# An fp32 two-block network on one core: the start's loads in halves and on a second queue, the shift as columns, the first expert activations ahead of the last score

## The chip, the core and the metric

The kernel runs on one core of one Trainium2 chip. Its engines are TensorE (PE; weight loads are listed apart as PEld), VectorE (DVE), ScalarE (ACT), GpSimd (POOL) and SyncE (SP), each with a queue of its own that it works off in order, and 16 DMA engines. SP, ACT and POOL issue DMAs. The metric is the device time in microseconds, the median of three runs.

## The reference, cut to what matters

Two blocks run one after the other in fp32 on 512 tokens of width 1024. The first has a modulation, windowed attention, a gated convolution and a mixture of 16384 experts of rank 1, of which each token takes 8 x 16. The second has two layers, each with a mixer, cross attention over a memory of 256 tokens, and an MLP. The parts that the change touches:

```python
# modulation: one row for the tokens (c), one for the context (c_ctx)
m = silu(cond) @ w_mod + b_mod            # shift, scale, gate, shift, scale, gate
h  = rmsnorm(x,  n1) * (1 + sc1)  + sh1
hc = rmsnorm(xc, n1) * (1 + csc1) + csh1
...
# experts
qh = (t @ w_q).reshape(T, 8, 2, 128)
s = einsum('thpd,hpnd->thpn', qh, sub_keys)   # scores of the sub-keys
s_top, i_top = top_k(s, 16)
...
act = gelu(einsum('thkd,td->thk', u_tab[idx], t))
y = einsum('thk,thkd->td', g * act, v_tab[idx])
...
# second block
kv = mem @ mem_w_kv                        # once, for both layers
o = softmax(q @ mem_k.T / 16) @ mem_v
x = layer_norm(ALPHA * x + o @ wo)
```

## The kernel before

**Products.** Every weight comes from HBM as fp32 into one of two buffers named `raw` (`wload`, L73; the load is L81) and is split into a high part `wh` and a rest `wl`: ACT casts (L68), DVE subtracts (L69), 1024 columns at a time. Activations are split in the same way. Each product then takes three matmuls, L93 to L95. In a transposed product (`fm`) the weights are the stationary operand, in the other (`tm`) the activations.

**Order.** The Python text names the operations; a scheduler then fixes each engine's own order, and semaphores join the engines. So the order of a queue differs from the order of the text, and an edit in one place can move rows of other engines. The DMAs that SP and ACT issue share eight semaphores in turn, so an issue can also wait for the DMA that had its semaphore before.

**The start.** The keys and values of the memory (`mem_kv`, c = 0 to 7, result `pskv`, copied to `kv` by ACT at L326 and stored) are computed while the modulation is loaded. The first product needs the split memory `mt` and the split weights of c = 0. Between the products stands a loop over four quarters. Each loads `w_mods` (1 MB) and `w_modh` (1 MB) into the two buffers `wm`. The scale comes from DVE: `gemv` at L217 multiplies `w_mods` by the broadcast rows `crow` and `ccrow` and adds up, four times a quarter. The shift comes from PE: L358 has `cc` (the two conditions, 2 columns) as stationary operand and streams 512 columns of `w_modh`, in two PSUM tiles `gv`. Then come `mem_kv(1 + c)` and 128 tokens of x: load, scaling by their norm on ACT, eight transposes into `psT` (L339), copies into `xn`. Behind the loop the shift's two rows are copied (`mrow`), turned into columns by eight transposes (`pssh`, L372), and `xn` is modulated on DVE (L344) and split into `h`. Then c = 5, 6, 7 (called kv5, kv6, kv7 below), the context, and the projections of the first block.

**The experts.** `score` makes, for each pair of a head and a half, the matmuls `pss` of queries `pq` (split) and keys, and transposes the scores (`psst`); DVE takes the 16 best (`top`). Behind the last `score`, a loop over c loads the table's rows `peer_u[c]`, multiplies them by `h` (`psu`), and writes gelu of it to HBM (`actd`, store at L791 on SP). Rows chosen by index come by indirect DMAs that POOL issues (`rows`, L749); DVE takes dot products with them at L732. Gates are placed by one-hot products (`oh`, L1049, and `pg`, L1025) and stored (`gd`, L1035 on SP). A DMA issue on SP holds up what stands behind it until its source is ready.

**Cross attention.** `xattn` runs four heads, then `tm_stage` loads the out-projection `xo` and multiplies (`tm`).

Of the kernel before, what the change touches and what calls it, by code (L numbers as in the profile page):

```python
# [9 lines left out]
F32 = mybir.dt.float32  # L10
F32R = mybir.dt.float32r
# [4 lines left out]
AF = mybir.ActivationFunctionType  # L16
# [4 lines left out]
P = 128  # L21
T = 512
NT = 4
D = 1024
KT = 8
# [6 lines left out]
ND = T - NG  # L32
NE = ND // P
WCOLS = 1032
# [8 lines left out]
class Net:  # L43
# [130 lines left out]
    def tm_stage(self, X, wsrc, evac, side, nwp=2):  # L174

        with self.pool("wx", side=side, bufs=8 - 2 * nwp) as wx:
            w = [self.wload(wsrc[c], wx if c >= nwp else None) for c in range(4)]
            for t in range(NT):  # L180
                for half in range(2):
                    ps = self.psa.tile([P, 512], F32, tag="a", name=f"tm{t}")
                    for c in range(2):
                        self.tm(ps, w[2 * half + c], X, t, nk=4, k0=4 * c, width=512, start=c == 0, stop=c == 1)
                    if half == 1:
                        self.flush()
                    evac(t, half, ps)
# [45 lines left out]
    def front(self):  # L233
# [53 lines left out]
        with self.pool("start", side="right") as sp, self.pool("start2", side="right", bufs=2) as sp2, \  # L287
# [16 lines left out]
            nc.sync.dma_start(crow, i["c"].partition_broadcast(P))  # L304
            nc.sync.dma_start(ccrow, i["c_ctx"].partition_broadcast(P))
            nc.scalar.activation(crow, crow, AF.Silu)
            nc.scalar.activation(ccrow, ccrow, AF.Silu)
            nc.sync.dma_start(modb, i["b_mod"])
            nc.sync.dma_start(bhc, i["b_row"])
            nc.sync.dma_start(b1c, i["b_col"])  # L310
            nc.sync.dma_start(n1c, i["norm1_g"])
            nc.sync.dma_start(n2c, i["norm2_g"])
            wm_es = ExitStack()
            wmp = wm_es.enter_context(self.pool("wm", side="right", bufs=2))
            gv = [self.psa.tile([P, 512], F32, tag="a", name=f"gv{b}") for b in range(2)]
            def mem_kv(c, pool, tag):
                w = w_kv.pop() if w_kv else self.wload(i["mem_w_kv"][c])
                ps = pool.tile([P, 512], F32, tag=tag, name="pskv")
                for j in range(2):
                    o = ps[:, j * 256 : (j + 1) * 256]  # L320
                    if c < 4:
                        self.fm(o, w, j, MT, cols=slice(0, 256))
                    else:
                        self.tm(o, w, MT, j)
# [22 lines left out]
            for c in range(4):  # L347
# [19 lines left out]
            mrow = sp2.tile([P, D], F32, tag="xt", name="mrow", bufs=3)[:2]  # L367
            for b in range(2):
                nc.scalar.copy(mrow[:, b * 512 : (b + 1) * 512], gv[b][:2])
            ps = self.psc.tile([P, 512], F32, tag="c", name="pssh")  # L370
# [264 lines left out]
    def peer(self):  # L635
# [38 lines left out]

        with self.pool("qk", side="right", bufs=2) as qp, self.pool("keys", side="right") as kp:
# [31 lines left out]
            for hp in range(16):  # L707
# [12 lines left out]
                last = (hp, q)  # L720
            score(*last)
# [57 lines left out]

        def u_matmuls(w, a, tile_):  # L780
            for j in range(2):
                ps = tile_()
                self.fm(ps[:, :ND], w, j, H2, cols=slice(0, ND))
                nc.scalar.activation(a[:, j * ND : (j + 1) * ND], ps[:, :ND], AF.Gelu)

        G0 = 12
        for c in range(C1):
            w = self.wload(i["peer_u"][c])
            a = uact.tile([P, 2 * ND], F32, tag="act", name="act")
            u_matmuls(w, a, lambda: self.psa.tile([P, 512], F32, tag="a", name="psu"))  # L790
            nc.sync.dma_start(actd[c], a)  # L791
# [146 lines left out]
    def routing(self, VAL, IDX, GT, iota_n, iota_a, first_a, u1, u2, gd, ids, gg):  # L938
# [81 lines left out]
        def expand(oh, gs, b, dst):  # L1020
# [13 lines left out]
            if b == 1:  # L1034
                nc.sync.dma_start(dst, gs.rearrange("p (b n) t -> p b (n t)", b=16))  # L1035
# [315 lines left out]
    def xattn(self, l):  # L1351
# [4 lines left out]
        with self.pool("xa", side=other, bufs=2) as xp, self.pool("xa4", side=other, bufs=4) as xp4:  # L1356
# [55 lines left out]
            for h in range(4):  # L1412
                p1 = scores(Q, kv, 1)
# [17 lines left out]
        self.tm_stage(O, i["xo"][4 * l : 4 * l + 4], evac, other)  # L1431
# [226 lines left out]
```

## Time and profile before

| | before |
|---|---|
| median of 3 runs | 2922.74 us (2921.97 to 2922.75) |
| the profiled execution's own time | 2922.15 us |
| its span in the trace | 2920.3 us |
| PE busy | 2878.6 us, 99% of the span |
| DVE, ACT, POOL busy | 69%, 44%, 13% |

The profile is of one execution. Its span leaves out 1.9 us around the program. Shares are means over stages that differ: 99% for PE says that the other engines are a limit only in the short stretches in which PE waits or has its lower clock.

### The profile page before, as it was taken

What the parts mean: (1) busy time and instruction counts of PE and PEld (TensorE: products, weight loads), DVE (VectorE), ACT (ScalarE), POOL (GpSimd) and SP (SyncE); (2) the same over time, 40 slices, a digit from 0 to 9 for tenths busy, and PEclk for the clock granted to TensorE, in tenths of its full rate; (3) what the DMA queues carried; (4) which work ended last, traced back from release to release, by engine and by line L of the source; (5) the groups of instructions that cost most, each with busy time, mean ns of one, the idle gap of its engine ahead of it and who ended that gap; (6) DMA issues with size and microseconds to landing.
All of it is one profiled execution on the core that took longest, in us unless ns stands there. A gap on an engine that the chain in (4) does not pass through costs nothing.

```text
span 2920.3 us, 39527 instructions
## 1 busy us (share of the span) xinstructions
PE 2878.6 (99%) x15409; PEld 2482.8 (85%) x15409; DVE 2016.5 (69%) x3823; ACT 1279.8 (44%) x1910; POOL 367.5 (13%) x283
## 2 busy tenths in 40 slices
PE   7999999999999999999999999999999999999998
PEld 5887888899999989988888889888888889888887
DVE  6887658989768688888888884766433456643345
ACT  5565334456556333333333365644433334433332
POOL 0000000000101355454444200000000000000000
PEclk9999999999999999999999999999999999999999
DMA  8312642257889999999999722223322222322221
GB/s 323 127 44 104 228 159 101 98 209 229 278 270 298 354 362 357 344 343 392 387 368 364 263 79 102 108 94 110 116 93 102 89 99 80 105 92 99 101 75 70
DMA packets 163402, 556.21 MB, mean 190 GB/s; under 512 B 13712, under 2 KB 62992, under 8 KB 131984
## 3 DMA queue, kind: packets, MB, share of 16 engines
q1 hardware_dynamic: 125200, 417.37, 40.1%
q0 software_dynamic: 36864, 134.23, 12.4%
q8 instruction: 120, 1.97, 0.3%
q10 hardware_dynamic: 1152, 2.10, 0.2%
q14 instruction: 66, 0.54, 0.1%
HBM read 504.90 MB, written 48.76 MB: 190 GB/s over the span
## 4 chain that ended last, share of the span: by engine, by line
PE 87%; DVE 6%; issue 3%; DMA 3%; ACT 1%; POOL 0%; SPq 0%; DVEq 0%; ACTq 0%; POOLq 0%
PE ps L95 8%; PE ps L93 8%; PE ps L94 8%; PE po L93 6%; PE po L94 6%; PE po L95 6%; PE psu L93 3%; PE psu L94 3%; PE psu L95 3%; PE tm L93 2%; PE tm L94 2%; PE tm L95 2%; PE pu L95 2%; PE pu L93 2%; PE pu L94 2%
## 5 line engine op out<-in xcount | busy, mean ns | idle before, releaser
L69 DVE TENSOR_TENSOR wl<-raw,wh 128x1024 fp32r<-128x1024 f32 x538 | 652.2, 1221 | 273.4 <-ACT wh L68 259.8
L68 ACT CAST wh<-raw 128x1024 fp32r<-128x1024 f32 x538 | 559.0, 1048 | 633.2 <-PE ps L95 228.5
L94 PE MATMUL po<-wl,ga 128*128 128x512 f32 x768 | 302.9, 394 | 0.0
L93 PE MATMUL po<-wh,ga 128*128 128x512 f32 x768 | 302.7, 394 | 0.0
L95 PE MATMUL po<-wh,ga 128*128 128x512 f32 x768 | 302.5, 394 | 0.0
L749 POOL DMA_INDIRECT rows<-in_u_rows,ids x128 | 171.6, 1341 | 599.2 <-DVE rows L732 398.7
L93 PE MATMUL psu<-h,wh 128*128 128x384 f32 x704 | 241.3, 343 | 0.0
L94 PE MATMUL psu<-h,wh 128*128 128x384 f32 x704 | 239.0, 339 | 0.0
L95 PE MATMUL psu<-h,wl 128*128 128x384 f32 x704 | 238.8, 339 | 0.0
L749 POOL DMA_INDIRECT rows<-in_peer_v,ids x128 | 186.1, 1454 | 229.9 <-DVE acc L742 216.3
L95 PE MATMUL ps<-wh,hg 128*128 128x512 f32 x512 | 201.8, 394 | 0.0
L93 PE MATMUL ps<-wh,hg 128*128 128x512 f32 x512 | 201.7, 394 | 0.0
L94 PE MATMUL ps<-wl,hg 128*128 128x512 f32 x512 | 201.2, 393 | 0.0
L68 ACT CAST ga<-m 128x384 fp32r<-128x384 f32 x128 | 65.5, 513 | 268.5 <-DVE m L835 120.6
L94 PE MATMUL ps<-xt,wh 128*128 128x512 f32 x448 | 176.9, 395 | 0.0
L93 PE MATMUL ps<-xt,wh 128*128 128x512 f32 x448 | 176.8, 395 | 0.0
L95 PE MATMUL ps<-xt,wl 128*128 128x512 f32 x448 | 176.5, 394 | 0.0
L95 PEld LDWEIGHTS po<-wh,ga 128*128 128x128 f32 x768 | 144.2, 188 | 34.1
L93 PEld LDWEIGHTS po<-wh,ga 128*128 128x128 f32 x768 | 144.1, 188 | 33.3
L94 PEld LDWEIGHTS po<-wl,ga 128*128 128x128 f32 x768 | 144.1, 188 | 33.2
L732 DVE SCALAR_TENSOR_TENSOR rows<-rows,hrow 128x1024 f32<-128x1024 f32 x128 | 154.8, 1219 | 20.4 <-DMA rows<-in_u_rows,ids 20.4
L742 DVE SCALAR_TENSOR_TENSOR acc<-rows,dots,acc 128x1024 f32<-128x1024 f32 x127 | 162.9, 1283 | 0.4
(542 smaller groups left out, 6651.5 us busy)
## 6 DMA issues: line engine op xcount, KB each, us to landing
raw<-in_peer_u SPq DMA_DIRECT2D x64, 1024.0 KB
raw<-in_peer_v SPq DMA_DIRECT2D x64, 1024.0 KB
raw<-in_w SPq DMA_DIRECT2D x64, 1024.0 KB
gd<-gs SPq DMA_DIRECT2D x24, 1024.0 KB
g<-gd SPq DMA_DIRECT2D x16, 1536.0 KB
raw<-in_w_in SPq DMA_DIRECT2D x17, 1024.0 KB
actd<-act SPq DMA_DIRECT2D x44, 384.0 KB
a<-actd SPq DMA_DIRECT2D x44, 384.0 KB
```

The source lines that it names most:

```text
L68: self.nc.scalar.copy(h, src)
L69: self.nc.vector.tensor_sub(l, src, h.bitcast(F32))
L93: mm(ps, a[0], b[0], start=start, stop=False)
L94: mm(ps, a[0], b[1], start=False, stop=False)
L95: mm(ps, a[1], b[0], start=False, stop=stop)
L732: keep(nc.vector.scalar_tensor_tensor(r, r, 1.0, self.hrow, op0=ALU.mult, op1=ALU.mult, accum_out=dots[:, j : j + 1]))
L742: keep(nc.vector.scalar_tensor_tensor(acc[0], r, dots[:, j : j + 1], acc[0], op0=ALU.mult, op1=ALU.add))
L749: nc.gpsimd.indirect_dma_start(out=r, out_offset=None, in_=i["u_rows"] if n < P else i["peer_v"], in_offset=bass.IndirectOffsetOnAxis(ap=i ...
```

## The change

Six edits. The memory and the first weights are loaded in two halves each, in turn on SP, and split half by half; the product c = 0 takes the halves in that order. The eight small loads (the conditions, also as broadcast rows, biases and norms) are issued by ACT. The shift is computed as columns: `w_modh` is the stationary operand, 128x128 at a time, and `cc` the two moving columns, in one PSUM tile, with no transposes behind. The first `u_matmuls` (c = 0) stand ahead of the last `score`. The stores of `act` and of the gates `gs` are issued by ACT. Two loads of `xo` are named inside the last head.

```diff
-    def tm_stage(self, X, wsrc, evac, side, nwp=2):
+    def tm_stage(self, X, wsrc, evac, side, nwp=2, w=()):
...
-            w = [self.wload(wsrc[c], wx if c >= nwp else None) for c in range(4)]
+            w = list(w) + [self.wload(wsrc[c], wx if c >= nwp else None) for c in range(len(w), 4)]
...
-            mraw = self.rawp.tile([P, 2048], F32, tag="raw", name="memt")
-            nc.sync.dma_start(mraw, i["mem"])
+            for dst, src in ((cc, "cc"), (modb, "b_mod"), (bhc, "b_row"), (b1c, "b_col"), (n1c, "norm1_g"), (n2c, "norm2_g")):
+                nc.scalar.dma_start(dst, i[src])
+            for dst, src in ((crow, "c"), (ccrow, "c_ctx")):
+                nc.scalar.dma_start(dst, i[src].partition_broadcast(P))
+
+            mraw, kraw = (self.rawp.tile([P, 2048], F32, tag="raw", name=nm) for nm in ("memt", "raw"))
+            w_kv = [[]]
             for j in range(2):
-                v = mraw[:, j * 1024 : (j + 1) * 1024].rearrange("p (k m) -> p k m", k=4)
+                js = slice(j * 1024, (j + 1) * 1024)
+                nc.sync.dma_start(mraw[:, js], i["mem"][:, js])
+                nc.sync.dma_start(kraw[:, js], i["mem_w_kv"][0][:, js])
+            for j in range(2):
+                js = slice(j * 1024, (j + 1) * 1024)
+                v = mraw[:, js].rearrange("p (k m) -> p k m", k=4)
                 self.split(MT[0][:, 4 * j : 4 * j + 4], MT[1][:, 4 * j : 4 * j + 4], v)
-            w_kv = [self.wload(i["mem_w_kv"][0])]
-            nc.sync.dma_start(cc, i["cc"])
+                w_kv[0].append(tuple(self.wp.tile([P, WCOLS], F32R, tag=f"w{z}", name=f"w{z}") for z in "hl"))
+                self.split(w_kv[0][j][0][:, :1024], w_kv[0][j][1][:, :1024], kraw[:, js])
...
+                if c == 0:
+
+                    for x in range(16):
+                        k, j = x // 8 * 4 + x % 4, x // 4 % 2
+                        s, (wh, wl) = slice(k % 4 * 256 + j * P, k % 4 * 256 + (j + 1) * P), w[k // 4]
+                        self.mm3(o[j], (wh[:, s], wl[:, s]), (MT[0][:, k], MT[1][:, k]), x == 0, x == 15)
+                for j in range(2 if c else 0):
...
-                for b in range(4):
-                    k = 2 * c + b // 2
-                    nc.tensor.matmul(gv[b % 2][:2], cc[:, k], raw[:, b * 512 : (b + 1) * 512], start=k == 0, stop=k == 7)
+                for b in range(16):
+                    k, f = 2 * c + b // 8, b % 8
+                    nc.tensor.matmul(
+                        gv[:, 2 * f : 2 * f + 2], raw[:, b * P : (b + 1) * P], cc[:, k], start=k + f == 0, stop=k + f == 14)
...
-            for k in range(KT):
-                nc.tensor.transpose(ps[:, 2 * k : 2 * k + 2], mrow[:, k * P : (k + 1) * P], self.ident[:2, :2])
-            nc.vector.tensor_add(shc, ps[:, :16].rearrange("p (k z) -> p k z", z=2), bhc[:, :, None].to_broadcast([P, 8, 2]))
+            nc.vector.tensor_add(shc, gv[:, :16].rearrange("p (k z) -> p k z", z=2), bhc[:, :, None].to_broadcast([P, 8, 2]))
...
+        def activations(c):
+            w = self.wload(i["peer_u"][c])
+            a = uact.tile([P, 2 * ND], F32, tag="act", name="act")
+            u_matmuls(w, a, lambda: self.psa.tile([P, 512], F32, tag="a", name="psu"))
+            nc.scalar.dma_start(actd[c], a)
...
+            activations(0)
             score(*last)
...
-            nc.sync.dma_start(actd[c], a)
+            if c:
+                activations(c)
...
-                nc.sync.dma_start(dst, gs.rearrange("p (b n) t -> p b (n t)", b=16))
+                nc.scalar.dma_start(dst, gs.rearrange("p (b n) t -> p b (n t)", b=16))
...
+                if h == 3:
+                    wo = [self.wload(i["xo"][4 * l + c]) for c in range(2)]
```

The edits move rows of the engines. The first place is DVE's queue around the copy of `xn` for the last quarter of x. Each `wl<-raw,wh` is the subtract of half a weight block. Before, from the last norm of x on:

```order
L69 TENSOR_TENSOR wl<-raw,wh 128x1024 x2
L162 TENSOR_SCALAR rms_850<-rms_ss 128x1
L361 COPY xn<-psT 128x4x128
L373 TENSOR_TENSOR shc<-pssh,bhc 128x16
L344 TENSOR_SCALAR xn<-xn,scc,shc 128x512 x6
L69 TENSOR_TENSOR h_114<-xn,h_113 128x1024 x3
L344 TENSOR_SCALAR xn<-xn,scc,shc 128x512 x2
L69 TENSOR_TENSOR wl<-raw,wh 128x1024 x2
L69 TENSOR_TENSOR h_114<-xn,h_113 128x1024
L69 TENSOR_TENSOR wl<-raw,wh 128x1024 x2
```

The first `wl` pair there is that of kv5, the others those of kv6 and kv7. The same place after the change:

```order
L165 SCALAR_TENSOR_TENSOR rms_651<-rms_652,rms_651 128x1
L370 COPY xn<-psT 128x4x128
L352 TENSOR_SCALAR xn<-xn,scc,shc 128x512 x6
L69 TENSOR_TENSOR h_114<-xn,h_113 128x1024 x3
L352 TENSOR_SCALAR xn<-xn,scc,shc 128x512 x2
L69 TENSOR_TENSOR wl<-raw,wh 128x1024 x2
L69 TENSOR_TENSOR h_114<-xn,h_113 128x1024
L69 TENSOR_TENSOR wl<-raw,wh 128x1024 x2
```

Now the pairs behind the copy are those of kv5 and kv6: kv5's has moved from ahead of the copy to behind the modulates, and PE has one product more to run behind them.

The second place is SP's queue in the loop over quarters; the semaphores in brackets name the engine that an issue waits for (DMAHW is one of the eight shared by the DMAs). Before, quarters 1 and 2:

```order
L349 DMA wm<-in_w_mods 128x2048 [waits DMAHW7_49,DMAHW2_49,DVE_49]
L355 DMA wm<-in_w_modh 128x2048 [waits DMAHW3_49,DMAHW0_49,PE_49]
L81 DMA raw<-in_mem_w_kv 128x2048 [waits DMAHW1_49,Activation_49]
L333 DMA xt<-in_x 128x1024
L349 DMA wm<-in_w_mods 128x2048 [waits DMAHW7_49,DMAHW4_49,DVE_49]
```

After:

```order
L81 DMA raw<-in_mem_w_kv 128x2048 [waits DMAHW3_49,DMAHW0_49,DVE_49]
L357 DMA wm<-in_w_mods 128x2048 [waits DMAHW5_49,DMAHW2_49,PE_49]
L363 DMA wm<-in_w_modh 128x2048 [waits DMAHW4_49,DVE_49]
L341 DMA xt<-in_x 128x1024
L81 DMA raw<-in_mem_w_kv 128x2048 [waits DMAHW6_49,DVE_49]
L357 DMA wm<-in_w_mods 128x2048 [waits DMAHW7_49,DMAHW3_49,PE_49]
```

The two buffers `wm` have changed roles from quarter to quarter: `w_mods` now takes the one that PE's `gv` frees, `w_modh` the one that DVE's `gemv` frees, and the next weights of the memory product (`raw`) stand ahead of the pair instead of behind it.

The third place is PE's queue at the last score. Before, the last `pss` stands three matmuls behind the transposes of the score before:

```order
L93 MATMUL pss<-pq_5471,kh_4394 128x512
L95 MATMUL psu<-h_3917,wl 128x384
L699 MATMUL psst<-ident,sf 128x128 x4
L93 MATMUL psu<-h_3917,wh 128x384
L94 MATMUL psu<-h_3918,wh 128x384
L95 MATMUL psu<-h_3917,wl 128x384
L94 MATMUL pss<-pq_5472,kh_4394 128x512
L95 MATMUL pss<-pq_5471,kl_4395 128x512
```

After, behind the transposes and the 41 `psu` matmuls that follow them:

```order
L93 MATMUL psu<-h_3954,wh 128x384
L94 MATMUL psu<-h_3955,wh 128x384
L95 MATMUL psu<-h_3954,wl 128x384
L93 MATMUL pss<-pq_5508,kh_4431 128x512
L94 MATMUL pss<-pq_5509,kh_4431 128x512
L95 MATMUL pss<-pq_5508,kl_4432 128x512
```

So all of the first `psu` block stands ahead of the last `pss` now. Behind this block PE's rows are the same as before, and from the cross attention on so are those of every engine but for the numbers of DMA semaphores.

## Rows read from the trace of the kernel before

**Rows 1.** The page: busy time, share, instructions.

```profile
PE 2878.6 (99%) x15409; PEld 2482.8 (85%) x15409; DVE 2016.5 (69%) x3823; ACT 1279.8 (44%) x1910; POOL 367.5 (13%) x283
```

**Rows 2.** What PE waited for: us in total, times, longest us.

```profile
PE pskv L93 <- ACT wh L68: 11.2, 3, 9.4
...
PE tm L93 <- ACT wh L68: 2.8, 2, 1.4
...
PE pss L94 <- DVE pq L69: 3.5, 2, 2.9
...
PE pg L1025 <- DVE oh L1049: 2.5, 3, 1.9
```

**Rows 3.** Table by stretches: us, busy of each engine, PEclk, DMA share, GB/s.

```profile
20.00:60.00 40.00, 35.69 (x208) 23.26 (x207) 28.91 (x55) 21.43 (x31) 0.00 (x0) 1.00 0.91 335
...
558.00:570.00 12.00, 9.07 (x44) 8.41 (x43) 11.50 (x63) 4.58 (x6) 0.00 (x0) 0.86 0.25 88
...
765.00:785.00 20.00, 17.71 (x113) 17.25 (x113) 17.15 (x28) 12.02 (x16) 3.97 (x3) 0.91 0.82 259
...
1000.00:1600.00 600.00, 600.00 (x2802) 514.73 (x2802) 512.77 (x657) 212.82 (x294) 289.40 (x204) 1.00 0.96 364
```

**Rows 4.** Timeline of the start: start us, us, engine, line, operation.

```profile
0.74 1.28 ACT L68 ACT_TABLE_LOAD   x1 [0.74 <-PEq L1648]
...
5.81 1.99 ACT L68 CAST mt<-memt 128x1024 fp32r<-128x1024 f32 x2 [3.79 <-DMA memt<-in_mem]
...
10.67 0.58 PE L95 MATMUL pskv<-mt,wl 128*128 128x256 f32 x1 [0.47 <-DVE wl L69]
...
18.80 0.59 ACT L326 COPY kv<-pskv 128x512 f32<-128x512 f32 x1 [5.08 <-PE pskv L95]
```

**Rows 5.** Timeline of PE: `gv`, `pssh`, and `psd` much later.

```profile
42.60 3.59 PE L358 MATMUL gv<-wm,cc 128*2 128x512 f32 x8
...
65.56 0.65 PE L372 MATMUL pssh<-ident,mrow 2*128 2x2 f32 x8
...
2402.25 0.29 PE L1525 MATMUL psd<-band,x 128*128 128x16 f32 x2
...
2402.70 0.29 PE L1525 MATMUL psd<-band,x 128*128 128x16 f32 x2
```

**Rows 6.** Timeline of the loop: `w_mods` issued on SP, first used on DVE.

```profile
32.49 0.33 SPq L349 DMA_DIRECT2D wm<-in_w_mods  x1
...
39.89 1.22 DVE L217 SCALAR_TENSOR_TENSOR junk<-wm,crow 128x1024 bf16<-128x1024 f32 x1 [1.67 <-DMA wm<-in_w_mods]
...
44.96 0.33 SPq L349 DMA_DIRECT2D wm<-in_w_mods  x1
...
49.78 1.23 DVE L217 SCALAR_TENSOR_TENSOR junk<-wm,crow 128x1024 bf16<-128x1024 f32 x1
```

**Rows 7.** Timeline behind the loop: PE, DVE and ACT.

```profile
64.59 1.03 PE L339 MATMUL psT<-ident,xt 128*128 128x128 f32 x8
...
73.61 2.35 DVE L69 TENSOR_TENSOR wl<-raw,wh 128x1024 fp32r<-128x1024 f32 x2
...
74.88 0.39 PE L94 MATMUL pskv<-wl,mt 128*128 128x256 f32 x1 [0.80 <-DVE wl L69]
...
86.31 0.59 ACT L326 COPY kv<-pskv 128x512 f32<-128x512 f32 x1 [0.55 <-PE pskv L95]
```

**Rows 8.** Timeline at the last score: DVE and PE.

```profile
546.60 1.20 DVE L69 TENSOR_TENSOR wl<-raw,wh 128x1024 fp32r<-128x1024 f32 x1
...
559.67 1.21 DVE L69 TENSOR_TENSOR wl<-raw,wh 128x1024 fp32r<-128x1024 f32 x1
...
561.53 0.50 PE L94 MATMUL pss<-pq,kh 128*128 128x512 f32 x1 [2.93 <-DVE pq L69]
```

**Rows 9.** What SP waited for, and DVE from 560 to 800 us.

```profile
SPq L791 <- ACT act L784: 181.5, 37, 11.2
...
DVE rows L732 <- DMA rows<-in_u_rows,ids: 17.3, 4, 7.7
```

More of the change, by code (lines that the diff above doesn't have):

```diff
@@ L300, in front @@
                 self.split(MT[0][:, 4 * j : 4 * j + 4], MT[1][:, 4 * j : 4 * j + 4], v)
-            w_kv = [self.wload(i["mem_w_kv"][0])]
-            nc.sync.dma_start(cc, i["cc"])
+                w_kv[0].append(tuple(self.wp.tile([P, WCOLS], F32R, tag=f"w{z}", name=f"w{z}") for z in "hl"))
+                self.split(w_kv[0][j][0][:, :1024], w_kv[0][j][1][:, :1024], kraw[:, js])
             nc.scalar.activation(cc, cc, AF.Silu)
-            nc.sync.dma_start(crow, i["c"].partition_broadcast(P))
@@ L305, in front @@
-            nc.sync.dma_start(ccrow, i["c_ctx"].partition_broadcast(P))
             nc.scalar.activation(crow, crow, AF.Silu)
             nc.scalar.activation(ccrow, ccrow, AF.Silu)
[L308 to L312, printed above, removed]
             wm_es = ExitStack()
             wmp = wm_es.enter_context(self.pool("wm", side="right", bufs=2))
-            gv = [self.psa.tile([P, 512], F32, tag="a", name=f"gv{b}") for b in range(2)]
+            gv = self.psa.tile([P, 512], F32, tag="a", name="gv")
@@ L318, in mem_kv @@
                 ps = pool.tile([P, 512], F32, tag=tag, name="pskv")
-                for j in range(2):
-                    o = ps[:, j * 256 : (j + 1) * 256]
+                o = [ps[:, j * 256 : (j + 1) * 256] for j in range(2)]
+                if c == 0:
[4 more added lines that the diff above has]
+                for j in range(2 if c else 0):
                     if c < 4:
-                        self.fm(o, w, j, MT, cols=slice(0, 256))
+                        self.fm(o[j], w, j, MT, cols=slice(0, 256))
                     else:
-                        self.tm(o, w, MT, j)
+                        self.tm(o[j], w, MT, j)
                 kv = sp2.tile([P, 512], F32, tag="kv", name="kv")
@@ L366, in front @@
             nc.vector.scalar_tensor_tensor(scc, scc, 1.0, n1c[:, None, :].to_broadcast([P, 2, 8]), op0=ALU.add, op1=ALU.mult)
[L367 to L370, printed above, removed]
-            for k in range(KT):
-                nc.tensor.transpose(ps[:, 2 * k : 2 * k + 2], mrow[:, k * P : (k + 1) * P], self.ident[:2, :2])
-            nc.vector.tensor_add(shc, ps[:, :16].rearrange("p (k z) -> p k z", z=2), bhc[:, :, None].to_broadcast([P, 8, 2]))
+            nc.vector.tensor_add(shc, gv[:, :16].rearrange("p (k z) -> p k z", z=2), bhc[:, :, None].to_broadcast([P, 8, 2]))
             for k in range(KT):
@@ L673, in top, with u_matmuls @@
                 self.top16(VAL[:, t, hp], IDX[:, t, hp], scs[hp][:, ts_], sc2)
+        def u_matmuls(w, a, tile_):
+            for j in range(2):
+                ps = tile_()
+                self.fm(ps[:, :ND], w, j, H2, cols=slice(0, ND))
+                nc.scalar.activation(a[:, j * ND : (j + 1) * ND], ps[:, :ND], AF.Gelu)
+        def activations(c):
[3 more added lines that the diff above has]
+            nc.scalar.dma_start(actd[c], a)
         with self.pool("qk", side="right", bufs=2) as qp, self.pool("keys", side="right") as kp:
@@ L778, in peer @@
         up = ExitStack()
[L780 to L784, printed above, removed]
         G0 = 12
         for c in range(C1):
-            w = self.wload(i["peer_u"][c])
-            a = uact.tile([P, 2 * ND], F32, tag="act", name="act")
-            u_matmuls(w, a, lambda: self.psa.tile([P, 512], F32, tag="a", name="psu"))
-            nc.sync.dma_start(actd[c], a)
+            if c:
+                activations(c)
             if c < LAG:
@@ L1429, in evac @@
                 self.ln(t, XT2)
-        self.tm_stage(O, i["xo"][4 * l : 4 * l + 4], evac, other)
+        self.tm_stage(O, i["xo"][4 * l : 4 * l + 4], evac, other, w=wo)
         oe.close()
```

## The prediction

> **What bounds the kernel now.** I read the page's summary first: TensorE (PE) is busy for 99% of the span [rows 1]. A change can therefore pay only where PE stands still or runs at half clock, or by giving PE fewer rows to run. Then the list of what PE waited for [rows 2]: the first weights (9.4 us of the 11.2 in the first row), the last score (2.9 us in one piece), the one-hot of the experts' gather (`oh`, 1.9 us in one piece) and two out-projections (1.4 us each). Then a table by stretches [rows 3], for the clock. In the 12 us that hold the score's wait the mean granted clock is 0.86: the wait is followed by a short time at 1.2 GHz instead of 2.4, and 12 x 0.14 = 1.7 us of clock are lost. The 20 us with the `oh` wait have 0.91, so 1.8 us. From 1000 to 1600 PE is never idle and the clock is whole: nothing is to be had there. A gap of 2 to 3 us thus costs about 1.7 us beyond itself here.
>
> **1. The first product.** Before, the cast of the memory starts at 5.81 us [rows 4], the first matmul at 9.4 [rows 2], the one that needs the subtracted half `wl` at 10.67, and the product is done at 18.80 [rows 4]. After, ScalarE (ACT) first issues eight loads. An issue takes 0.33 us on SP [rows 6], so eight take 2.6 us or somewhat more; with the table load of 1.28 us from 0.74 [rows 4] the first cast begins between 4.6 and 6.0, about where it began before. But now one cast of 1 us (two took 1.99) for the memory and one for the weights are enough: first matmul at about 8.0, and one subtract of some 1.2 us later `wl` at about 9.4. That is 1.2 us sooner, so the product is done at about 17.6. The other bound: 1 MB of the two broadcast rows now travels beside the memory instead of behind it. The DMA engines are at a share of 0.91 and 335 GB/s from 20 to 60 us [rows 3], so 1 MB is 3.1 us, and if all of it goes ahead of the second halves, the product ends 1.9 us later than before. I take the 1.2 us, since the first halves are issued before those rows. A rule speaks for the other end: the Trainium skill, "DMA: Bandwidth & Descriptors", section "Issuing engines are not separate DMA queues", says that DMAs from several engines run on the same 16 engines and interleave, and that another issuing engine saves only issue time. The share of 0.91 agrees; by that rule taken strictly the sum below would be 2927.0 instead of 2923.9.
>
> **2. The shift as columns.** Before, each of four quarters runs four matmuls of 512 moving columns, 3.59 us [rows 5]. After, it runs 16 matmuls with 128x128 fp32 weights and two moving columns. Not shown before; the nearest row is `psd`, with the same weights and 16 columns: from one L1525 to the next is 0.45 us [rows 5], in which an L1525 and an L1523 run with two rows each, so 0.11 us a row. 16 x 2 x 0.11 = 3.6 us: **nothing is saved**. The low end is `pssh`, whose loads have 2x128 elements: 8 in 0.65 us [rows 5], 0.08 a row, 2.6 us a quarter, 4 us less over four. I take 3.6, because weights of `psd` are the same in shape and type. The eight transposes that go (0.65 us) and two small copies on ACT are within the error.
>
> **3. The loop over quarters.** The order of the queue shows that a load of `w_mods` now waits for PE's `gv` of the quarter before, and not for VectorE (DVE). So the period is: landing of `w_mods`, then of `w_modh` 1 MB behind it (3.1 us), then `gv` (3.6). A landing took 7.4 us (32.49 to 39.89) and 4.8 (44.96 to 49.78) [rows 6]. Period 11.5 to 14.1; I take 12.2, nearer the short one, as the load of `mem_w_kv` has been issued earlier in the new order. `gv` of quarter 0 ends at 17.6 + 3.6 = 21.2, of quarter 3 at 21.2 + 3 x 12.2 = 57.8. Then follow 35 matmuls of `pskv` at 0.12 (95 matmuls from 74.88 to 86.31 [rows 7]), 4.2 us, and 2.7 us of copy, scaling and eight transposes `psT`: they end at 64.7, against 64.59 + 1.03 = 65.6 before [rows 7]. **-0.9 us**, with bounds of 62.6 and 70.4 (-3.0, +4.8), and -7.0 with the low `gv`.
>
> **4. Behind the last transposes.** Before, DVE made kv5's two `wl` ahead of the copy of `xn`, so PE ran `pskv` of c = 5 under DVE's copy, modulates and subtracts, and stood still only for what was left. DVE came to kv6's `wl` at 73.61; the first matmul that needs it ran at 74.88, 9.3 us after `psT`, and c = 7 was done 20.7 us after `psT` [rows 7]. After, the order has kv5's `wl` behind those same instructions. PE can do two matmuls, then waits: 9.3 us until the `wl`, then 142 matmuls at 0.12 = 17.0, together 26.3 us after `psT`. **+5.6 us.** Queued behind the waiting matmul are all of kv5 to kv7, the context's transposes and the K projection, so nothing on PE fills it. The wait is longer than all but the first of [rows 2], so I add a clock loss: **+1.7 us** (0 at the other end). Start in all: -0.9 + 5.6 + 1.7 = **+6.4**. Low end -7.0 + 5.6 = -1.4; high end 4.8 + 3.1 for the later first product + 5.6 + 1.7 = +15.2.
>
> **5. The last score.** Before, `pss` L94 waited 2.9 us for DVE's subtract of `pq` [rows 2, 8], because two `wl` of the next weights stood ahead of it (the second from 559.67). After, 41 matmuls of `psu` stand between, some 7 us, and their own weights were split 11 us before (546.60) [rows 8]; by the time that PE is back at the score, `pq` is there. The gap and its clock loss go: -2.9 - 1.7 = **-4.6**. Other end 0, if PE only comes to a later wait sooner.
>
> **6. Stores on ACT's queue.** SP waited 181.5 us for `act` [rows 9], and also for `gs`, with weight loads behind them; those loads now go earlier. ACT gets 68 issues at about 0.33 us, 22 us, spread over 560 to 1000, where it is busy for 12 of 20 us [rows 3] and PE hardly waits for it: nothing. If that cover is gone, or if a third queue slows the gathers, for which DVE already waits 17.3 us [rows 9], the `oh` wait grows; if the earlier loads leave the gathers alone, that wait and its clock loss go. I take 0, ends -4.0 (1.9 + 0.4 + 1.7) and +4.0.
>
> **7. Out-projections.** The weights are named earlier, but the order of every engine from there on is what it was: the 1.4 us waits [rows 2] stay. 0.
>
> **Sum.** +6.4 - 4.6 = +1.8 on the profiled execution's 2922.15: 2923.9; that execution is 0.6 below the median of the runs, so **2924.5**. All low ends together give 2912, all high ends 2941.
>
> **Rivals.**
> A. *The start gains.* If a load with two columns costs as little as `pssh`, the loop shortens, and with short landings the start is -1.4; with -4.6 for the score that is 2916, and 2912 without the `oh` wait. For it: the first product is sooner and PE's share is only 0.89 from 20 to 60 us [rows 3]. Against it: `psd`'s spacing, and the 9.3 us, which do not depend on either. Here too a page speaks: the Trainium skill, "TensorE: Matmul & The Clock Gate", section "Back-to-back issue gap", states a floor near 25 ns between starts of small matmuls; if it held with a weight load for each, a quarter would take 0.8 us, an estimate by that page, and with 11 us less over four quarters the time would be 2913. No run here shows such a spacing, and `psd` contradicts it. Chance 0.17.
> B. *The clock falls in the loop (slower).* For 3.6 us in each quarter PE streams two columns behind each load; before it streamed 512. If the clock falls to 1.2 GHz after each of the four, that is 4 x 1.7 = 6.8 more: 2931. It decides from the third such fall on. For it: both waits in [rows 3] were followed by one. Against: PE isn't idle meanwhile, and part of it hides behind landings. Chance 0.21.
> C. *The score's gain is given back.* If DVE is the bound up to the `oh` wait, PE arrives there 4.6 us sooner and waits 4.6 longer: 2929.1. Against: DVE itself waits for gathers before that place [rows 9], so it isn't full. The edits 6 and 7 then do nothing either. Chance 0.12.
> My forecast, 2919 to 2928, has 0.5.
>
> **How the numbers follow.** A change under 0.2% (5.8 us) cannot be told from none here. Faster by more (below 2916.9): A, 0.17. Slower by more (above 2928.6): B and half of C, 0.27. Same: the rest, 0.56. The range takes in A's 2916 to 2912 in part and B: 2914 to 2932.
>
> **What would show it.** In the profile after: first matmul near 8.0; `gv` 3.6 us a quarter; `psT` of quarter 3 ending near 64.7; a wait of `pskv` L94 for `wl` of 8 to 9 us, followed by a lower clock; c = 7's copy near 92; no wait of `pss` L94 and a clock of 1.00 there; `oh` and out-projection waits as before. I am wrong if that `pskv` wait is short (an order that hides it), if `gv` takes under 3 us, or if gathers land much later.

## The result, and the profile after

The changed kernel takes 2938.6 us (median of 6 runs, 2935.1 to 2944.6) against 2922.4 of the kernel before on the same chip: a ratio of 1.0061, interval 1.0051 to 1.0071. It is 16 us slower, outside the range that was forecast (2914 to 2932), and it scatters over 9.5 us where these six runs of the kernel before scatter over 2.4 (the larger sets below, 23 to 33 runs of it, scatter over 7 to 10).

The span of the profiled execution is 2935.7 us, 15.4 more than before. What PE waited for in it (us in total, times, longest), to be read against [rows 2]:

```profile
PE pskv L93 <- ACT wh L68: 17.7, 5, 10.3
PE psT L347 <- ACT xt L342: 3.4, 2, 1.7
PE pskv L94 <- DVE wl L69: 3.4, 2, 2.5
...
PE tm L93 <- ACT wh L68: 3.0, 3, 1.4
PE pg L1032 <- DVE oh L1056: 2.1, 2, 1.7
...
PE pss L94 <- DVE pq L69: 0.6, 1, 0.6
```

The wait of the last score is gone, those of the one-hot and of the out-projections are as they were. What was lost lies in the start, with the memory's products (`pskv`) and the transposes of x (`psT`). The table by stretches (us, busy time of PE, PEld, DVE, ACT and POOL, granted clock, DMA share, GB/s), against [rows 3]:

```profile
20.00:60.00 40.00, 35.99 (x252) 34.87 (x251) 23.45 (x45) 17.11 (x25) 0.00 (x0) 0.83 0.78 298
60.00:90.00 30.00, 17.66 (x105) 16.29 (x106) 19.45 (x34) 16.75 (x24) 0.00 (x0) 0.74 0.39 144
...
558.00:580.00 22.00, 22.00 (x108) 18.09 (x107) 21.86 (x121) 10.10 (x15) 0.00 (x0) 1.00 0.22 82
765.00:800.00 35.00, 32.92 (x242) 32.25 (x241) 24.28 (x39) 22.82 (x29) 3.76 (x3) 1.00 0.77 248
```

From 20 to 60 us PE is as busy as before, but its mean granted clock is 0.83 where it was 1.00; from 60 to 90 it is 0.74, and PE stands still for 12 of 30 us. The same view, cut where the clock changes, for the five stretches at 1.2 GHz (called falls below):

```profile
23.24:30.07 6.83, 6.07 (x29) 5.81 (x28) 4.18 (x9) 6.13 (x8) 0.00 (x0) 0.50 0.95 332
...
50.55:57.37 6.82, 6.82 (x34) 6.82 (x34) 1.73 (x7) 0.00 (x0) 0.00 (x0) 0.50 0.46 161
...
64.20:67.60 3.40, 3.40 (x17) 3.40 (x18) 3.26 (x5) 0.86 (x3) 0.00 (x0) 0.50 0.30 87
...
71.03:74.44 3.41, 3.41 (x18) 3.41 (x18) 3.31 (x11) 0.00 (x0) 0.00 (x0) 0.50 0.78 294
...
81.27:91.51 10.24, 3.74 (x16) 3.45 (x17) 10.24 (x13) 8.50 (x13) 0.00 (x0) 0.50 0.10 22
```

They add up to 30.7 us, in which PE is busy for 23.4; at 2.4 GHz that work would have taken half, so by that estimate 11.7 us are lost to the clock. The kernel before has no such stretch between 20 and 130 us. The timeline says what PE did ahead of each (start, duration, engine, line, operation, in brackets the idle time and what ended it; the row at 67.86 holds the last 25 of the 32 matmuls of quarter 3, which end at 70.8):

```profile
19.47 3.63 PE L366 MATMUL gv<-cc,wm 128*128 128x2 f32 x32
...
35.04 3.63 PE L366 MATMUL gv<-cc,wm 128*128 128x2 f32 x32
...
48.41 4.88 PE L366 MATMUL gv<-cc,wm 128*128 128x2 f32 x32
...
60.55 1.09 PE L347 MATMUL psT<-ident,xt 128*128 128x128 f32 x8 [1.72 <-ACT xt L342]
62.83 0.38 PE L93 MATMUL pskv<-wh,mt 128*128 128x256 f32 x1 [1.18 <-ACT wh L68]
64.09 0.50 PE L94 MATMUL pskv<-wl,mt 128*128 128x256 f32 x1 [0.88 <-DVE wl L69]
67.86 2.93 PE L366 MATMUL gv<-cc,wm 128*128 128x2 f32 x25
...
78.28 1.09 PE L347 MATMUL psT<-ident,xt 128*128 128x128 f32 x8 [1.72 <-ACT xt L342]
80.56 0.39 PE L93 MATMUL pskv<-wh,mt 128*128 128x256 f32 x1 [1.19 <-ACT wh L68]
85.29 0.58 PE L93 MATMUL pskv<-wh,mt 128*128 128x256 f32 x1 [4.34 <-ACT wh L68]
88.35 0.58 PE L94 MATMUL pskv<-wl,mt 128*128 128x256 f32 x1 [2.48 <-DVE wl L69]
```

The falls at 23.24, 50.55 and 71.03 come within or right behind the shift matmuls of quarters 0, 2 and 3; those at 64.20 and 81.27 behind waits of 3.8 and 2.9 us. Behind quarter 1's (35.04) there is none. The waits of 1.7 us for `xt` have a reason in ACT's order:

```profile
58.87 0.58 ACT L334 COPY kv<-pskv 128x512 f32<-128x512 f32 x1 [8.47 <-PE pskv L95]
59.35 1.15 ACT L342 ACTIVATE xt<-xt,rms 128x1024 f32<-128x1024 f32 x1
```

The scaling of `xt` stands behind the copy of the memory's product and so waits until PE has finished it; PE then waits for the scaling (again at 77.08). In the last quarter of the kernel before, of the columns alone and of the rows again (both runs below), the scaling stands ahead of that copy, and PE doesn't wait there.

The last transposes end at 79.4 instead of 65.6, and the copy of c = 7, the last row of [rows 7], is at 106.85 instead of 86.31: the start is 20.5 us longer. Some 4.5 us come back by the one-hot wait, which ends at 791.26 us, 16.0 after that of the kernel before (775.22), most of it at the last score.

The first product, against [rows 4]:

```profile
0.74 0.41 ACTq L296 DMA_DIRECT2D cc<-in_cc  x1
...
5.12 0.34 ACTq L298 DMA_DIRECT2D crow<-in_c  x1
6.56 0.33 ACTq L298 DMA_DIRECT2D ccrow<-in_c_ctx  x1
6.92 1.28 ACT L68 ACT_TABLE_LOAD   x1 [6.92 <-DMA modb<-in_b_mod]
8.22 1.04 ACT L68 CAST mt<-memt 128x1024 fp32r<-128x1024 f32 x1
...
14.40 1.05 ACT L68 CAST wh<-raw 128x1024 fp32r<-128x1024 f32 x1 [3.25 <-DMA raw<-in_mem_w_kv]
...
19.67 0.58 ACT L334 COPY kv<-pskv 128x512 f32<-128x512 f32 x1 [0.79 <-PE pskv L95]
```

ACT's last two issues went out at 5.12 and 6.56, since each waits for the semaphore of an earlier load (those of `cc` and `modb`); the table load and the first cast stand behind them, the cast 2.4 us later than before, and the product is done 0.9 us later.

### The profile page after: what moved, and what is told of

The parts are those of the page before. It is cut to its first block, busy times and chain, and to the rows that moved or that the text cites. A ratio compares the mean times of both kernels' runs of the same rounds, so it can differ in the third digit from the quotient of the medians.

```text
span 2935.7 us, 39651 instructions
## 1 busy us (share of the span) xinstructions
PE 2885.2 (98%) x15497; PEld 2500.1 (85%) x15497; DVE 2015.9 (69%) x3823; ACT 1276.5 (43%) x1908; POOL 373.6 (13%) x283
## 3 DMA queue, kind: packets, MB, share of 16 engines
q0 software_dynamic: 36864, 134.23, 12.2%
## 4 chain that ended last, share of the span: by engine, by line
PE 88%; DVE 5%; issue 3%; DMA 2%; ACT 1%; POOL 0%; ACTq 0%; DVEq 0%; POOLq 0%
PE ps L95 8%; PE ps L93 8%; PE ps L94 8%; PE po L95 6%; PE po L94 6%; PE po L93 6%; PE psu L93 3%; PE psu L95 3%; PE psu L94 3%; PE tm L94 2%; PE tm L93 2%; PE tm L95 2%; PE pu L95 2%; PE pu L94 2%; PE pu L93 2%
## 5 line engine op out<-in xcount | busy, mean ns | idle before, releaser
L94 PE MATMUL po<-wl,ga 128*128 128x512 f32 x768 | 302.9, 394 | 0.0
L765 POOL DMA_INDIRECT rows<-in_u_rows,ids x128 | 178.8, 1397 | 587.6 <-DVE rows L748 382.8
L94 PE MATMUL psu<-h,wh 128*128 128x384 f32 x704 | 237.9, 338 | 0.0
L94 PE MATMUL ps<-wl,hg 128*128 128x512 f32 x512 | 201.2, 393 | 0.0
L94 PE MATMUL ps<-xt,wh 128*128 128x512 f32 x448 | 176.9, 395 | 0.0
L94 PEld LDWEIGHTS po<-wl,ga 128*128 128x128 f32 x768 | 144.1, 188 | 33.1
```

Of the source, the lines that this page charges most:

```text
L94: mm(ps, a[0], b[1], start=False, stop=False)
L765: nc.gpsimd.indirect_dma_start(out=r, out_offset=None, in_=i["u_rows"] if n < P else i["peer_v"], in_offset=bass.IndirectOffsetOnAxis(ap=i ...
```

## The experiments

Each run was compared with the kernel before on its own chip; ratios with their 95% interval. A new name `ccw` stands for the conditions `cc` repeated side by side. Half-clock time is from the profiled execution of each run.

**1. One part undone, two parts alone, and the disputed operation changed in itself.**

*The shift as rows again, all else as in the changed kernel.*

```diff
-                for b in range(16):
-                    k, f = 2 * c + b // 8, b % 8
-                    nc.tensor.matmul(
-                        gv[:, 2 * f : 2 * f + 2], raw[:, b * P : (b + 1) * P], cc[:, k], start=k + f == 0, stop=k + f == 14)
+                for b in range(4):
+                    k = 2 * c + b // 2
+                    nc.tensor.matmul(gv[b % 2][:2], cc[:, k], raw[:, b * 512 : (b + 1) * 512], start=k == 0, stop=k == 7)
```

> The changed kernel with the shift computed as rows again (512 moving columns, then eight transposes); all other edits stay. Theory (the clock falls because of the two-column matmuls): from 20 to 75 us the granted clock stays at 2.4 GHz but for a fall behind a long wait, and the time is 2918 to 2924 us. Rival (the order is to blame: the next weights' subtract behind the modulates, the memory's halves landing late): the falls stay and the time is 2930 us or more.

Measured 2919.6 us, 0.9996 (0.9987 to 1.0005). A row of its table by stretches:

```profile
20.00:60.00 40.00, 39.45 (x245) 27.51 (x244) 30.49 (x61) 23.65 (x35) 0.00 (x0) 1.00 0.95 371
```

And its one long wait, from the timeline of PE:

```profile
70.75 0.58 PE L94 MATMUL pskv<-wl,mt 128*128 128x256 f32 x1 [6.68 <-DVE wl L69]
```

The clock is whole up to 60 us; the only stretch at 1.2 GHz before 130 us begins within that wait (6.8 us). Without one edit out of six the whole loss is gone: 1.0061 against 0.9996 is 19 us. Orders change with it too, ACT's scaling of `xt` among them, so this run alone does not say how much of the 19 is the clock.

*The shift as columns alone, in the kernel before* (the reverse of that diff, and `shc` read from `gv` without transposes).

> The kernel before with the shift as columns as its only edit; kv5's subtracts stay ahead of the copy of xn. Theory (clock): falls to 1.2 GHz between 20 and 75 us, time 2930 to 2936 us. Rival (order): no falls before 130 us, time within 3 us of the kernel before, 2920 to 2925 us.

Measured 2932.2 us, 1.0039 (1.0025 to 1.0053), 11 us more than before.

```profile
20.00:60.00 40.00, 38.03 (x251) 37.14 (x250) 23.64 (x46) 17.41 (x25) 0.00 (x0) 0.74 0.68 268
60.00:90.00 30.00, 25.91 (x192) 25.31 (x191) 23.37 (x45) 20.17 (x28) 0.00 (x0) 0.89 0.73 264
```

The shift of quarters 0 and 1 in its timeline (3.63 us each at the full clock):

```profile
18.15 4.48 PE L358 MATMUL gv<-cc,wm 128*128 128x2 f32 x32 [0.25 <-DMA wm<-in_w_modh]
...
31.46 4.23 PE L358 MATMUL gv<-cc,wm 128*128 128x2 f32 x32 [0.73 <-DMA wm<-in_w_modh]
```

DVE's order around the copy of `xn` is that of before (kv5's subtracts ahead of it), PE is busier than before from 20 to 60, and still the clock is 0.74: 27.3 us at 1.2 GHz between 20 and 90, in which PE is busy for 26.1, so some 13.0 us lost by the same estimate, against 11.2 measured. Three of the five falls begin within the shift matmuls of quarters 0, 1 and 2 (at 20.9, 34.5 and 51.6), and PE's waits from the first of them up to there are under 0.8 us each. So the clock falls with the columns, without the order of DVE that step 4 of the prediction goes by.

*The first expert activations alone, in the kernel before.*

```diff
+            activations(0)
             score(*last)
...
-            w = self.wload(i["peer_u"][c])
+            if c:
+                activations(c)
```

> The kernel before with the first expert activations ahead of the last score as its only edit. Theory: the wait of 2.9 us and the clock loss of 1.7 us behind it go and nothing takes their place: 4 to 5 us less than before, 2917.5 to 2918.5 us. Rival (given back at the one-hot wait): within 1 us of the kernel before, and the one-hot wait longer by some 4 us.

Measured 2915.5 us, 0.9983 (0.9974 to 0.9992), 5.5 us less. What PE waited for in it:

```profile
PE pg L1030 <- DVE oh L1054: 2.5, 3, 1.9
...
PE pss L94 <- DVE pq L69: 0.6, 1, 0.6
```

And the stretch of the last score in its table by stretches:

```profile
553.00:575.00 22.00, 22.00 (x122) 20.67 (x122) 21.80 (x112) 10.54 (x14) 0.00 (x0) 1.00 0.32 114
```

The wait and the fall behind it are gone, the one-hot wait is as long as before: nothing is given back.

*64 columns in the changed kernel:* the same weights, but 32 copies of the two conditions stream.

```diff
+            ccw = wmp.tile([P, KT, 64], F32, name="ccw", bufs=1)
+            nc.gpsimd.tensor_copy(ccw.rearrange("p k (a z) -> p k a z", z=2), cc[:, :, None, :].to_broadcast([P, KT, 32, 2]))
...
-                        gv[:, 2 * f : 2 * f + 2], raw[:, b * P : (b + 1) * P], cc[:, k], start=k + f == 0, stop=k + f == 14)
+                        gv[:, 64 * f : 64 * f + 64], raw[:, b * P : (b + 1) * P], ccw[:, k], start=k + f == 0, stop=k + f == 14)
```

> The changed kernel with the two conditions repeated to 64 moving columns, of which two are used; each shift matmul has the same weights. Theory (what counts for the clock is what PE streams): the 32 rows of a quarter still take 3.6 us, the falls between 20 and 60 us go, and the time is 2922 to 2927 us. Rival (waits and weight loads make it fall, whatever is streamed): falls as in the changed kernel, 2933 us or more.

Measured 2925.2 us, 1.0016 (1.0005 to 1.0026).

```profile
20.00:60.00 40.00, 36.89 (x300) 35.87 (x299) 30.65 (x54) 21.48 (x31) 0.00 (x0) 0.97 0.88 347
60.00:90.00 30.00, 23.05 (x151) 22.61 (x152) 19.92 (x40) 19.14 (x25) 0.00 (x0) 0.76 0.46 169
```

More streaming takes hardly longer (3.68 us a quarter) and wins back 13 us of the 19; but the scheduler also moved one of kv5's subtracts ahead of the copy here, and ACT's scalings of `xt` ahead of other rows, so the order isn't quite the same, and from 57 us on there are still two stretches at 1.2 GHz. It needed a cleaner pair.

**2. The other edits.**

*Halves and ACT's issues alone, in the kernel before.*

```diff
+            for dst, src in ((cc, "cc"), (modb, "b_mod"), (bhc, "b_row"), (b1c, "b_col"), (n1c, "norm1_g"), (n2c, "norm2_g")):
+                nc.scalar.dma_start(dst, i[src])
...
+                nc.sync.dma_start(mraw[:, js], i["mem"][:, js])
+                nc.sync.dma_start(kraw[:, js], i["mem_w_kv"][0][:, js])
...
```

> The kernel before with only the memory and first weights in halves and the eight small loads on ScalarE's queue. Theory (ScalarE's issues stand ahead of the first cast, and the order behind the loop is worse): first matmul near 10.2 instead of 9.4 us, a wait of some 6 us for kv5's subtract with a clock loss behind it, time 2 to 5 us above the kernel before. Rival (the halves help, as the prediction's first step has it): first product 1 us sooner and time 1 us or more below.

Measured 2925.6 us, 1.0011 (1.0002 to 1.0020), 3 to 4 us more. The timeline has the first matmul at 10.33 us and, behind the last transposes,

```profile
72.20 0.58 PE L94 MATMUL pskv<-wl,mt 128*128 128x256 f32 x1 [6.67 <-DVE wl L69]
```

with 10.2 us at 1.2 GHz around it. The prediction's first step had this edit gain 1.2 us. Here one of kv5's two subtracts stands behind the modulates, with the shift still as rows: a move of kv5's subtracts comes with this edit already, and not with the columns alone.

*The stores on ACT's queue alone.*

```diff
-                nc.sync.dma_start(dst, gs.rearrange("p (b n) t -> p b (n t)", b=16))
+                nc.scalar.dma_start(dst, gs.rearrange("p (b n) t -> p b (n t)", b=16))
...
-            nc.sync.dma_start(actd[c], a)
+            nc.scalar.dma_start(actd[c], a)
```

> The kernel before with only the stores of act and gs moved to ScalarE's queue. Theory (hidden): within 1.5 us of the kernel before, with SP's wait for act gone. Rival (a third queue slows the gathers, or relieves them): the one-hot wait of 1.9 us grows, or goes with its clock loss, and the time moves by 3 to 4 us.

Measured 2922.2 us, 1.0002 (0.9993 to 1.0011). The one-hot wait is 1.8 us, DVE's wait for gathers about what it was. Hidden, as forecast.

*The first activations and both stores, in the old start.*

> The kernel before with the first expert activations ahead of the last score and both stores on ScalarE's queue; the start is that of before. Theory: the gain of the first edit alone (5 us in its run) and nothing from the stores, so 4 to 6 us below the kernel before. Rival (the two edits meet in the gathers): less than 3 us below.

Measured 2917.0 us, 0.9986 (0.9977 to 0.9995): the gain of the activations, and nothing from the stores that can be measured.

*The first activations, and the halves with the small loads on SP behind them* (the six small and two broadcast loads issued by SP after the second halves).

> The first expert activations ahead of the last score, and the memory and first weights in halves, but with the small loads behind them on SP's queue as before. Theory (it was ScalarE's issues that delayed the first cast): first cast near 5 and first matmul near 7 us, and the order behind the loop is as before, so 5 to 8 us below the kernel before. Rival (the halves themselves land no sooner, or the gain waits at the quarters' loads): first matmul sooner or not, but c = 7 done near 83 us as without halves, and 4 to 6 us below, no better than the first activations alone.

Measured 2917.1 us, 0.9985 (0.9976 to 0.9994), no better than the activations alone. The timeline shows why the theory was only half right:

```profile
7.20 0.58 PE L93 MATMUL pskv<-mt,wh 128*128 128x256 f32 x1 [7.20 <-ACT wh L68]
...
18.42 1.97 PE L367 MATMUL gv<-wm,cc 128*2 128x512 f32 x3 [2.51 <-DMA wm<-in_w_modh]
```

The first matmul comes 2.2 us sooner than before, as it should without ACT's issues ahead. Then PE waits 2.5 us for `w_modh`: the first weights were not what held the loop. A fall to 1.2 GHz of 3.4 us follows that wait, another a wait of 2.2 us for the next `w_modh`.

**3. The cleaner pair, and the order behind the loop.**

*64 columns in the old order.* PE's and SP's orders are those of the run with columns alone; ACT makes its first copy of `kv` ahead of the first scaling of `xt` instead of behind it.

> The kernel before with the shift as columns, but the conditions repeated to 64 moving columns: every engine's order is that of the run with columns alone, and only what a shift matmul streams differs. Theory (the two-column stretches let the clock fall): no falls between 20 and 60 us and a time within 3 us of the kernel before, 10 us or more below columns alone. Rival (the new form's order or its weight loads): falls and 2930 us or more, as columns alone.

Measured 2928.8 us, 1.0024 (1.0015 to 1.0032).

```profile
20.00:60.00 40.00, 36.41 (x276) 35.41 (x276) 26.26 (x52) 18.56 (x26) 0.00 (x0) 0.87 0.84 306
60.00:90.00 30.00, 25.95 (x193) 25.35 (x193) 20.92 (x39) 21.95 (x30) 0.00 (x0) 0.89 0.66 239
```

Between the two theories: 17 us at 1.2 GHz instead of 27, and 7 us slower than before instead of 11. The longer of its two falls (10.2 us) comes behind a shift that had waited 2.4 us for `w_modh`. That left open whether the form with 128x128 weights loses clock by itself, and led to the run with 128 columns below.

*The next weights ahead, in the changed kernel.*

```diff
+                if c == 3:
+                    w_kv.append(self.wload(i["mem_w_kv"][5]))
                 for ks, v in transposed(i["x"][c]):
```

> The changed kernel with the weights of c = 5 loaded and split ahead of the last quarter's transposes, so that their subtract stands ahead of the copy of xn again. Theory (in the changed kernel columns cost 17 us, of which 11 are the clock and the rest this wait and the fall behind it): the wait of 9 us behind the last transposes goes, falls between 20 and 60 us stay, 4 to 8 us below the changed kernel. Rival (it is all the clock's fall in the loop): within 2 us of the changed kernel.

Measured 2933.9 us, 1.0046 (1.0032 to 1.0059), about 4 us below the changed kernel, but the intervals overlap, and the runs fall into two groups: three at 2927.6 to 2929.6 with a mean granted clock of 0.995 and three at 2938.2 to 2938.3 with 0.992. In the profile, of one of the first three, the wait of 8.0 us behind the last transposes shrinks to 1.84 us in one piece, and six falls up to 93 us stay (23.9 us). So the wait may be a part of the loss; how large a part, these runs don't settle.

*64 columns in the old order, with the first activations.*

> The first expert activations ahead of the last score, and the shift as 64 columns in the old order. Theory: the gain of the first (5 us) and nothing lost by the second, 4 to 6 us below the kernel before. Rival (falls in the loop after all): no better than the kernel before.

Measured 2922.7 us, 1.0005 (0.9996 to 1.0014): the rival. What the activations win, 64 columns lose. The start is that of the run with 64 columns above, yet its profiled execution has 10.2 us at 1.2 GHz before 130 us instead of 17, and a mean clock of 0.96 from 20 to 60 us instead of 0.87; the wait for `w_modh` ahead of quarter 1's shift was 1.1 us instead of 2.4.

*The next weights ahead, with the first activations, in the old start.*

> The first expert activations ahead of the last score, in the old start, with the weights of c = 5 loaded and split a step sooner. Theory (the waits of 2.3 us behind the last transposes are for c = 6, whose subtract moves up with it): 1 to 3 us below the first activations alone. Rival (the memory's order shifts another wait there): no better than the first activations alone, about 5 us below the kernel before.

Measured 2917.1 us, 0.9987 (0.9979 to 0.9996): the rival again, no better than the activations alone; the waits behind the last transposes are 1.5 and 2.0 us instead of 1.8 and 0.9.

**4. What was still open.**

*128 columns in the old order* (as with 64; the results fill the two `gv` tiles).

> The kernel before with the shift as columns and the conditions repeated to 128 moving columns, in the old order of stages; the weights and their loads are those of the runs with 2 and 64 columns. Theory (the clock falls by what PE streams in the shift's stretches and their neighbourhood, so more columns mean less of it): a quarter's matmuls take 3.6 to 3.7 us, less time at 1.2 GHz before 100 us than the 17 us with 64 columns, and 2920 to 2926 us. Rival (the form with 128x128 weights loses the clock whatever it streams): 17 us or more at 1.2 GHz and 2928 us or more, as with 64.

Measured 2922.7 us, 1.0009 (1.0000 to 1.0017).

```profile
20.00:60.00 40.00, 35.78 (x290) 34.92 (x290) 28.94 (x55) 20.92 (x28) 0.00 (x0) 0.96 0.90 334
60.00:90.00 30.00, 27.20 (x216) 26.80 (x215) 22.25 (x44) 22.51 (x31) 0.00 (x0) 0.94 0.62 215
```

Two stretches of 3.4 us at 1.2 GHz are left, behind waits of 1.9 and 2.8 us; among the runs with the old start and the shift as rows, the profiled execution of the kernel before has none up to 130 us, that of the stores alone has one and that of the activations with both stores has two. A quarter takes 3.74 us at the full clock:

```profile
44.59 3.74 PE L360 MATMUL gv<-ccw,wm 128*128 128x128 f32 x32
```

The weights are the same with 2, 64 and 128 columns, and so is SP's order; PE's differs in one place (with 128, the eight transposes of one quarter stand ahead of the last eight shift matmuls), ACT's in the place of a copy and a cast. By medians the time is 11, 7 and 2 us above the kernel before. The intervals of 2 and of 128 columns lie apart (1.0025 to 1.0053, 1.0000 to 1.0017); neighbours overlap. The mean clock from 20 to 60 us is 0.74, 0.87 and 0.96, of one execution each, and the second run with 64 columns has 0.96 too, so the traces don't tell 64 from 128. The form with 128x128 weights does not cost the clock by itself: with 128 columns streamed behind the same weights instead of two, most of the loss is gone.

*The shift as rows and the next weights ahead, all else as in the changed kernel.*

> The changed kernel with the shift as rows again and the weights of c = 5 loaded and split a step sooner. Theory (what the new start still loses in the run with rows again is the wait of 6.7 us behind the last transposes with its clock loss): that wait shrinks below 3 us, and the time is 2 to 4 us below that run, level with the first activations alone (0.9983 of before). Rival (it is the later first product): the time stays near 0.9996 of before.

Measured 2917.7 us, 0.9992 (0.9983 to 1.0000). The wait shrank only in part:

```profile
75.15 0.58 PE L94 MATMUL pskv<-wl,mt 128*128 128x256 f32 x1 [4.09 <-DVE wl L69]
```

The time lies between the two theories and within both intervals: what the new start costs without columns, some 3 us, is not split further.

## Why the prediction was wrong

**The clock in the loop: step 3 put it at nothing, and rival B was too small.** The sum has one clock loss in the start, the 1.7 us of step 4, and that one came: 3.7 us of busy time at 1.2 GHz from 81.27 on, so 1.9 lost. In the loop it has none; a rival with a chance of 0.21 had four falls of 1.7, 6.8 us, and against it stood "PE isn't idle meanwhile". The four stretches before the last transposes hold 19.7 us of busy time at 1.2 GHz, so 9.9 us lost, and three of the four begin at the shift matmuls. The columns alone cost 11.2 us in a kernel that shares nothing else with the change, and 128 columns in place of two take away most of it. That the falls come with the two streamed columns is shown by these runs, whose orders are nearly the same; why the clock falls there, no run shows. The wide scatter of the changed kernel's times goes with the clock too: the mean granted clock of its runs is 0.995 at 2935.1 us, 0.994 at 2937.5 and 0.992 at 2944.5 and 2944.6. In which stretches it differs from run to run is not known, since the trace is of one execution.

**Step 2, right in its number and read wrongly.** A quarter's shift takes 3.63 us, 0.113 a row, as `psd` had it (3.6). The floor of 25 ns that was quoted for rival A, the Trainium skill, "TensorE: Matmul & The Clock Gate", section "Back-to-back issue gap", does not describe this stream: the section gives it for single matmuls, without a weight load for each, and the spacing here is 0.113 us. But "nothing is saved" stopped at the duration. The same 3.6 us had been 512 streamed columns at a time, and were now two.

**Step 3, the period of the loop, failed.** Forecast 12.2 us (11.5 to 14.1) from landings; the ends of the shift matmuls at 23.1, 38.7, 53.3 and 70.8 give 15.6, 14.6 and 17.5. The load of `w_mods` is issued as the shift of the quarter before ends, as the step has it (23.13 us). But landings were not what bound the period: no shift matmul waits for a DMA in this trace. The first period has 6.8 us at 1.2 GHz, the second waits of 2.1 us in all for casts and subtracts and a fall within its shift; in the third PE waits 3.8 us for the scaled `xt`, the cast and the subtract, one after another, and runs at 1.2 GHz ahead of them and behind. So the last transposes ended 13.8 us later than before, where the step had 0.9 earlier. Of these 14.7 us, 2.1 come from step 1, some 9.9 from the clock, and 2.7 are left for such waits.

**Step 4, the wait behind the transposes, right in length and end.** Forecast 9.3 us from their end to the first matmul with `wl`; measured 88.35 - 79.37 = 9.0. But it is not one wait for the subtract: PE waits 1.2 and 4.3 us for ACT's two casts of the same weights, with one matmul after each, and only the last 2.5 us for DVE. The prediction's sign, 8 to 9 us of `pskv` L94, doesn't appear as such. From there c = 7 ended 27.5 us after the transposes; the step's 26.3 and its 1.7 of clock make 28.0.

**Step 1, wrong by 2.1 us and in its cause.** It counted the issues at 0.33 us each; ACT's first six took 0.41 to 0.66, and the last two waited for semaphores until 5.12 and 6.56 us. The product came 0.9 us later, not 1.2 earlier. What PE waited for were the issues themselves: they stood ahead of ACT's first cast (8.22 instead of 5.81), and without them the first matmul came at 7.2 us. The second half of the weights was late as well (cast at 14.40, against 9.38 in the run with the small loads behind the halves), but PE never waited for it. The rule of the Trainium skill, "DMA: Bandwidth & Descriptors", section "Issuing engines are not separate DMA queues", had the right sign (1.9 us later); by the trace, PE's time was lost to the issues on ACT and their waits for earlier loads, and not to a late second half.

**Step 5, right.** -4.6 forecast, -5.5 measured alone (interval 2.3 to 7.6 less). Rival C, given back, is refuted. **Steps 6 and 7, right:** nothing from the stores; both out-projection waits are still 1.4 us. Clock falls that the kernel before has behind the last score's and the one-hot's waits were missing in this execution. No run has the two loads of `xo` alone.

**The sum.** The single edits measure +11.2 (columns), +4.1 (start), -5.5 (activations) and +0.7 (stores), together +10.5 by medians; the whole change measures +16.2. The rest comes where columns meet the new start: taking the columns out of the changed kernel wins 19 us, not 11. By the estimates above the clock costs about the same in both (11.7 us in the changed kernel, 13.0 with the columns alone), so the rest should lie in waits. Those for the scaled `xt` are in the changed kernel and in neither of the other two; what they and the wait for c = 5 are worth has not been measured alone.

Of all kernels tried, the four that have the first activations, the shift as rows and no load issued by ACT are the fastest (0.9983 to 0.9987 of before); they can't be told from one another, and the activations alone are the simplest of them.

## What to carry to other kernels

Before a matmul is turned round, look at what it streams as well as how long it takes: here a stretch of weight loads with two moving columns lasted as long as the old one (3.63 us against 3.59) and cost 11 us through the clock. Read the order of every engine behind an edit and follow the chain of waits from row to row; a period made of landings alone missed the clock, and the scaling, cast and subtract between them. And take a bundle apart before keeping it: here one of six edits was worth 5 us and another cost 11.

## What the runs showed of the hardware that was not expected

PE's granted clock fell to 1.2 GHz while PE was busy: in the changed kernel it is 0.50 from 50.55 to 57.37 us with 6.82 us busy, the shift matmuls ending at 53.3 within it; PE's last wait before, of 0.6 us, had ended at 47.83. With 2, 64 and 128 moving columns behind the same fp32 weights a quarter took 3.63, 3.68 and 3.74 us at the full clock. And a wait of the same kind is not always followed by a fall. The table by stretches of the kernel before has a whole clock around the waits behind its last transposes (1.5 and 0.8 us):

```profile
60.00:90.00 30.00, 27.70 (x235) 27.12 (x234) 23.52 (x48) 23.34 (x32) 0.00 (x0) 1.00 0.67 224
```

The run with the stores alone has the same start and the same two waits there (1.5 and 0.8 us), and this row:

```profile
60.00:90.00 30.00, 27.70 (x222) 27.11 (x222) 22.08 (x44) 23.25 (x32) 0.00 (x0) 0.94 0.64 212
```
